# Four reorderings around the stage turns of a hybrid decoder step, and weight steps behind more output units

## The chip, the cores and the metric

The kernel runs on one NeuronCore of a Trainium2 chip. The metric is the device time of one execution in microseconds; lower is better. Before the change it was 2583.95 us (median of 3 runs, 2576.30 to 2586.48 us).

## The reference

One inference step of a decoder trunk of two layers, over 512 prompt tokens and 64 sample tokens (576 columns) with a model width of 1024. All data is fp32.

```python
for l in range(2):
    x = x + 0.5 * gate1 * ffn1(modulate(rmsnorm(x)))     # silu(h Wa) * (h Wb), then W_dn; 2816 wide
    m = mixer(modulate(rmsnorm(x)))                      # one input projection, three branches, W_o
    x = x + gate2 * m
    x = x + 0.5 * gate3 * ffn2(modulate(rmsnorm(x)))
y = rmsnorm(x)
# mixer: sigmoid(ga) * W_A(b * conv3(c * xa)) + sigmoid(gb) * W_B(u * spatial_gate(layernorm(gelu(v))))
#        + sigmoid(gc) * scale * grouped(trailing_mean_w(p) - p), w in (2, 4, 8, 16)
```

Shift, scale and gate come from a projection of a conditioning vector (`w_ada`). Also returned are the last conv and pooling rows and the normalised v rows.

## The kernel before, in words

All work is laid out with features on the 128 partitions and tokens on the free axis, in two halves of 288 columns (256 prompt, 32 sample; h = 0 and h = 1). A product in fp32 is made of three matmuls of a faster type: every operand is split in a high part (`whi`, `hhi`: a rounding copy on ScalarE, ACT) and a low part (`wlo`, `hlo`: a subtraction on VectorE, DVE), and `wlo*hhi + whi*hlo + whi*hhi` is summed in PSUM on TensorE (PE). A *unit* (`units`) is one output block of 128 features and 288 tokens; its bank is then taken over ("evacuated") by ACT or DVE. Most input projections run as *groups* (`Groups.group`): two blocks by two halves in seven products in place of eight, with sums of weight blocks and sums of input blocks (the *moving sums* T1 to T4: `t_sum`, `t_split`, tiles `u`, `thi`, `tlo`).

**What sets the order.** The program is recorded in the order in which the code calls it, with no scheduler: each engine takes its instructions strictly in that order and waits where an operand or a buffer isn't ready. Three counters put side work between products. `beat()` runs what `later(n, f)` has put off by n beats (one per unit or product); `tick()` runs what `after(n, f)` has put off by n units (a product of a group counts a half). `W` holds the weights: raw tiles of 1 MB land by DMA in two buffers, and one *step* at a time splits a block into one of six pairs of buffers (`W.split`, `W.go`, `W.take`), as far as buffers are free. For a group a raw tile takes eight steps: S1 and S3 on GpSimd (POOL; `whi` L360, `raw` L356), S2 and S4 on DVE (`whi`, `raw` L356), and the splits a, c, b, d.

**The turn.** Between two stages the normalisation needs the sum of squares over all 1024 features. `end_stage` ends with four units on h = 0 and four on h = 1. `xupd` evacuates a unit into x (DVE L797 to L805), `square` squares it on ACT and adds it to `accsq`: on POOL, the eighth on DVE (L570). `norm1` sums over partitions on PE (L578) and raises to -1/2 on POOL (L582), `norm2` makes diagonals on DVE (L591 to L593), `norm_bc` spreads them by a matmul with ones (L597), `norm3t` makes the normalised halves: `u` on DVE (L630 to L634), `hhi` on ACT (L637, L639), and in its second part, put off to `run_lo`, `u` on ACT (L645) and `hlo` on DVE (L647). `start_stage` begins with two units on h = 0 whose products with `hlo` come last (`late`, L477), in whose middle (`mid`) h = 1 is normalised; then a third unit, the same on h = 1, a fourth weight block on both halves, and the groups. `t_late` puts off the third and fourth moving sums to the first group's products. There are five turns: into mixer 0, FFN 2 of layer 0, FFN 1 of layer 1, mixer 1 and FFN 2 of layer 1.

Elsewhere in the mixer, `ypair` makes the output projections of branches A and B: four units of four k-blocks for one weight pair. The steps of the `w_ada` projection (`ada_mm`, four matmuls at L514) are spread by `after`.

In a group, ACT copies the first product's bank to `pd` (L749), the third's to `pe` (L760), the fourth's to `pu` (L764); DVE adds the second, fifth and sixth to them (L753, L768, L773). The fourth product writes the bank that `pd` is read from, the fifth the one that `pe` is read from. SiLU of `pd` (L922) is on ACT between them.

Of the kernel before, what the change touches and what calls it, by code (L numbers as in the profile page):

```python
# [15 lines left out]
KT = D // P  # L16
DEPTH = 2
NTOK = 576
HALF = 288
# [16 lines left out]
def kernel(  # L36
# [7 lines left out]
    nc = tc.nc  # L44
# [386 lines left out]
    W = Weights()  # L431
# [23 lines left out]
        while pend:  # L455
            pend.pop(0)[1]()

    def units(specs, hooks={}, late=False, w=1, still=False):


        bk = [balloc() for _ in specs]
        K = specs[0][2]
        for k in range(K):
            for b, (slot, w0, _, rhs, _) in zip(bk, specs):
                whi, wlo = wk(slot, w0 + k)
                rhi, rlo = rhs(k)
                o = b[:, :HALF]
                nc.tensor.matmul(o, wlo, rhi, start=(k == 0), stop=False)  # L468
                if not late:
                    nc.tensor.matmul(o, whi, rlo, start=False, stop=False)  # L470
                nc.tensor.matmul(o, whi, rhi, start=False, stop=(k == K - 1 and not late))  # L471
            if k in hooks:
                hooks[k]()
        if late:
            for k in range(K):
                for b, (slot, w0, _, rhs, _) in zip(bk, specs):
                    nc.tensor.matmul(b[:, :HALF], wk(slot, w0 + k)[0], rhs(k)[1], start=False,  # L477
                                     stop=(k == K - 1))
        for b, s in zip(bk, specs):
            s[4](b)  # L480
            brelease(b)
        if not still:
            beat()
        tick(len(specs) * w)
# [71 lines left out]
    accsq = [None, None]  # L556
    nsq = [0, 0]
    rst = [None, None]

    def square(m, h):  # L560
        c0 = h * HALF
        src = xv(m, slice(c0, c0 + HALF))
        if nsq[h] % 8 == 0:
            accsq[h] = qalloc("accsq")
            nc.scalar.activation(accsq[h], src, AF.Square)
        else:
            s = qalloc("sq")
            nc.scalar.activation(s, src, AF.Square)
            eng = nc.vector if nsq[h] % 8 == 7 else nc.gpsimd
            eng.tensor_add(accsq[h], accsq[h], s)  # L570
            qrelease(s)
        nsq[h] += 1

    def norm1(h):
        nb = nrmbank()
        a = accsq[h]
        for j, c in enumerate((0, 128, 160)):
            nc.tensor.matmul(nb[:, j:j + 1], a[:, c:c + P], inv_d, start=True, stop=True)  # L578
        qrelease(a)
        ve = tmp("ve", 4, 2)  # L580
        nc.vector.tensor_scalar_add(ve[:, :3], nb[:, :3], EPS)
        nc.gpsimd.tensor_tensor(out=ve[:, :3], in0=ve[:, :3], in1=mhalf[:, :3], op=ALU.pow)  # L582
        rst[h] = ve
# [99 lines left out]

    def t_late(n=4):

        for n, (i, f) in enumerate(((3, t_sum), (3, t_split), (4, t_sum), (4, t_split))[:n]):
            for q in range(2):
                later(n + 1, lambda i=i, q=q, f=f: f(i, q))

    def t_free():  # L690
        for i in (1, 2, 3):
# [124 lines left out]
    def start_stage(l, sub, evac, last=4):  # L816

        s = [W.take() for _ in range(2)]

        def mid():  # L820
            norm1(1)
            run_lo(1)
            W.lows()
            run_lo()
            norm2(1)
            norm_ut(1, l, sub)

        run_lo(2)
        units([(s[i], 0, KT, hk(0), evac(i, 0)) for i in (0, 1)], {6: mid}, True)
        nb = norm_bc(1, nrmbank())  # L830
        late_lo.extend(norm3t(1, l, sub, nb))
        s.append(W.take())
        units([(s[2], 0, KT, hk(0), evac(2, 0))])
        run_lo()
        todo = t_early()
        todo.insert(4, lambda: W.pay("AD", 1))

        def some(n):
            for _ in range(min(n, len(todo))):
                todo.pop(0)()  # L840

        units([(s[i], 0, KT, hk(1), evac(i, 1)) for i in (0, 1)], {k: lambda: some(1) for k in range(KT)},
              True)
        W.hold = False
        W.pay()
        W.done()
        W.done()
        units([(s[2], 0, KT, hk(1), evac(2, 1))], {k: lambda: some(1) for k in range(KT)})
        W.done()
        s.append(W.take())  # L850
        some(99)
        for h in (1, 0):
            units([(s[3], 0, KT, hk(h), evac(3, h))])
        W.done()
        t_late(last)

    def end_stage(K, rhs, evac, nxt, first=None):
# [29 lines left out]
        for i in range(4):  # L887
            units([(s[i], 0, K, rhs(1), evac(4 + i, 1))],
                  {K - 1: turn1} if i == 0 else {2: turn3} if i == 2 else
                  {2: lambda: part3(4, 2)} if i == 3 else {})  # L890
            W.done()
            if i == 3:
                part3(6, 2)
            if i == 0:
                W.pay("AD+", 1)

# [103 lines left out]
    def mixer(l, nxt):  # L1000
# [204 lines left out]
        def ypair(rhs, evac, m, first=None):  # L1205
            s = W.take()
            for i in (0, 1):
                for h in (0, 1):
                    units([(s, 4 * i, 4, rhs(h), evac(m + i, h))])
                    if first is not None:  # L1210
                        first()
                        first = None
# [673 lines left out]
```

## Time and profile before

| | |
|---|---|
| time, median of 3 runs (range) | 2583.95 us (2576.30 to 2586.48) |
| time of the profiled execution | 2581.12 us |
| its span | 2579.4 us |
| PE busy | 2499.5 us, 97% |
| DVE busy | 1792.8 us, 70% |
| ACT busy | 1159.0 us, 45% |
| POOL busy | 782.6 us, 30% |
| DMA queue q1 | 300.52 MB, 35.1% of 16 engines |

The span is from the first to the last instruction; 1.7 us of the profiled time lie outside it. Busy shares are means over the whole span. The places where PE waits are few and short, and a list of PE's waits with the engine that ended each says more than the shares.

### The profile page before, as it was taken

The page shows a single profiled execution, that of the slowest core. Times are in us where ns is not written, and L with a number is a line of the kernel's source. Part 1 is how long each engine was busy: PE and PEld are TensorE (multiplying, and loading weights), DVE is VectorE, ACT ScalarE, POOL GpSimd, SP SyncE. Part 2 cuts the span into 40 slices and gives each one's busy share as a digit, 9 for nine tenths or more (in the row PEclk, how much of TensorE's full clock was granted, in tenths as well). Part 3 has the DMA queues.
Part 4 walks back from the last instruction along what each step waited for, and adds up shares of the span by engine and source line. Part 5 has one row for each costly group of instructions (what it writes and reads, how often), then busy time and mean ns, then how long its engine had stood idle before and what let it go on. Part 6 is the DMA issues. An engine that isn't in the chain of part 4 may idle for free. (4 is left out here: it accounts for less than half of the span.)

```text
span 2579.4 us, 46614 instructions
## 1 busy us (share of the span) xinstructions
PE 2499.5 (97%) x18604; PEld 2396.4 (93%) x18604; DVE 1792.8 (70%) x3201; ACT 1159.0 (45%) x2134; POOL 782.6 (30%) x878
## 2 busy tenths in 40 slices
PE   7999999999899999999999999999989999999998
PEld 4898999999899989999988999999989999999998
DVE  5766667666797486766776667766678966776675
ACT  5344335544445354333553344446444544453353
POOL 1233332221442223333222333422125232233230
PEclk9999999999999999999999999999999999999999
DMA  7554533312223334342324453332222331222222
GB/s 243 193 177 171 196 106 110 122 56 87 95 82 116 119 117 146 125 161 97 110 83 164 152 176 132 99 127 85 94 73 85 102 135 46 86 99 83 99 79 82
DMA packets 260551, 303.50 MB, mean 118 GB/s; under 512 B 10836, under 2 KB 215948, under 8 KB 260318
## 3 DMA queue, kind: packets, MB, share of 16 engines
q1 hardware_dynamic: 260334, 300.52, 35.1%
q8 instruction: 147, 2.41, 0.4%
q14 instruction: 70, 0.57, 0.1%
HBM read 292.75 MB, written 7.97 MB: 117 GB/s over the span
## 5 line engine op out<-in xcount | busy, mean ns | idle before, releaser
L324 DVE TENSOR_TENSOR wlo<-raw,whi 128x1024 fp32r<-128x1024 f32 (+2 forms) x578 | 639.6, 1114 | 210.1 <-ACT whi L320 200.8
L320 ACT ACTIVATE whi<-raw 128x1024 fp32r<-128x1024 f32 (+2 forms) x578 | 495.6, 866 | 237.6 <-PE mm L471 100.8
L722 PE MATMUL mm<-hhi,wlo 128*128 128x288 f32 x1920 | 571.7, 298 | 23.3 <-ACT pe L760 10.3
L724 PE MATMUL mm<-hhi,whi 128*128 128x288 f32 x1920 | 566.4, 295 | 0.0
L723 PE MATMUL mm<-hlo,whi 128*128 128x288 f32 x1920 | 566.3, 295 | 0.0
L468 PE MATMUL mm<-ghi,wlo 128*128 128x288 f32 x1408 | 418.7, 297 | 0.0
L471 PE MATMUL mm<-ghi,whi 128*128 128x288 f32 x1408 | 414.9, 295 | 0.0
L470 PE MATMUL mm<-glo,whi 128*128 128x288 f32 x1408 | 414.9, 295 | 0.0
L722 PEld LDWEIGHTS mm<-hhi,wlo 128*128 128x128 f32 x1920 | 361.3, 188 | 48.8 <-ACT pe L760 13.5
L724 PEld LDWEIGHTS mm<-hhi,whi 128*128 128x128 f32 x1920 | 361.5, 188 | 0.0
L723 PEld LDWEIGHTS mm<-hlo,whi 128*128 128x128 f32 x1920 | 361.5, 188 | 0.0
L722 PE MATMUL mm<-thi,wlo 128*128 128x288 f32 x1120 | 333.3, 298 | 2.6 <-ACT pd L749 2.6
L360 POOL TENSOR_TENSOR whi<-raw 128x512 f32<-128x512 f32 x120 | 174.0, 1450 | 522.8 <-DMA raw<-in_w_in_dram 138.4
L723 PE MATMUL mm<-tlo,whi 128*128 128x288 f32 x1120 | 330.4, 295 | 0.0
L724 PE MATMUL mm<-thi,whi 128*128 128x288 f32 x1120 | 329.4, 294 | 0.0
L797 DVE SCALAR_TENSOR_TENSOR x<-mm,mod,x 128x256 f32<-128x256 f32 x336 | 161.1, 480 | 218.7 <-PE mm L471 218.6
L468 PEld LDWEIGHTS mm<-ghi,wlo 128*128 128x128 f32 x1408 | 264.1, 188 | 17.8 <-issue 16.8
L470 PEld LDWEIGHTS mm<-glo,whi 128*128 128x128 f32 x1408 | 264.3, 188 | 0.2
L471 PEld LDWEIGHTS mm<-ghi,whi 128*128 128x128 f32 x1408 | 264.2, 188 | 0.0
L722 PEld LDWEIGHTS mm<-thi,wlo 128*128 128x128 f32 x1120 | 210.0, 187 | 15.4 <-issue 4.2
L724 PEld LDWEIGHTS mm<-thi,whi 128*128 128x128 f32 x1120 | 210.8, 188 | 0.0
L723 PEld LDWEIGHTS mm<-tlo,whi 128*128 128x128 f32 x1120 | 210.3, 188 | 0.0
(315 smaller groups left out, 4692.0 us busy)
## 6 DMA issues: line engine op xcount, KB each, us to landing
raw<-in_w_gu_dram SPq DMA_DIRECT2D x88, 1024.0 KB
ada<-in_w_ada_dram SPq DMA_DIRECT2D x256, 256.0 KB
raw<-in_w_in_dram SPq DMA_DIRECT2D x48, 1024.0 KB
raw<-in_w_dn_dram SPq DMA_DIRECT2D x52, 512.0 KB
raw<-in_w_dn_dram SPq DMA_DIRECT2D x24, 768.0 KB
adap<-in_w_ada_dram SPq DMA_DIRECT2D x32, 256.0 KB
raw<-in_w_o_dram SPq DMA_DIRECT2D x8, 1024.0 KB
xd<-x SPq DMA_DIRECT2D x16, 288.0 KB
```

Source lines behind the costliest of these rows:

```text
L320: nc.scalar.activation(hi, src, AF.Copy)
L324: eng.tensor_sub(lo, src, hi.bitcast(F32))
L360: nc.gpsimd.tensor_add(v4(self.sums[r][0])[:, 0], a21, a22)
L468: nc.tensor.matmul(o, wlo, rhi, start=(k == 0), stop=False)
L470: nc.tensor.matmul(o, whi, rlo, start=False, stop=False)
L471: nc.tensor.matmul(o, whi, rhi, start=False, stop=(k == K - 1 and not late))
L722: nc.tensor.matmul(o, wlo, rhi, start=(start and k == 0), stop=False, skip_group_check=True)
L723: nc.tensor.matmul(o, whi, rlo, start=False, stop=False, skip_group_check=True)
L724: nc.tensor.matmul(o, whi, rhi, start=False, stop=(k == 3), skip_group_check=True)
L797: nc.vector.scalar_tensor_tensor(out=xc, in0=ps[:, :PH], scalar=mod[:, gidx + m, 0:1], in1=xc, op0=ALU.mult, op1=ALU.add)
```

## The change

The diff has four parts. (a) In `square` the eighth sum is put in a list; for h = 1 it is recorded behind the last piece of `norm3t`, for h = 0 in `norm1`. (b) In `mid`, the low part of the third weight block (`W.lows`) is recorded behind the diagonals, and that block's first unit takes its products with `wlo` last (`late="w"`). (c) `t_late` spreads the third and fourth moving sums and their splits over seven beats in place of four. (d) `W.go()` runs one more weight step behind each unit of the fourth block in `start_stage` and behind each unit in `ypair`. In `units`, the new line `w, r = ...` assigns to `w`, which is also the parameter that weighs the unit in `tick(len(specs) * w)` at the function's end: behind a unit with `late="l"` it is 0, with `late="w"` it is 1.

```diff
-    def units(specs, hooks={}, late=False, w=1, still=False):
+    def units(specs, hooks={}, late="", w=1, still=False):
...
-                nc.tensor.matmul(o, wlo, rhi, start=(k == 0), stop=False)
-                if not late:
-                    nc.tensor.matmul(o, whi, rlo, start=False, stop=False)
+                if late != "w":
+                    nc.tensor.matmul(o, wlo, rhi, start=(k == 0), stop=False)
+                if late != "l":
+                    nc.tensor.matmul(o, whi, rlo, start=(late == "w" and k == 0), stop=False)
                 nc.tensor.matmul(o, whi, rhi, start=False, stop=(k == K - 1 and not late))
...
-                    nc.tensor.matmul(b[:, :HALF], wk(slot, w0 + k)[0], rhs(k)[1], start=False,
+                    w, r = (0, 1) if late == "l" else (1, 0)
+                    nc.tensor.matmul(b[:, :HALF], wk(slot, w0 + k)[w], rhs(k)[r], start=False,
...
-            eng = nc.vector if nsq[h] % 8 == 7 else nc.gpsimd
-            eng.tensor_add(accsq[h], accsq[h], s)
-            qrelease(s)
+            def add(eng):
+                eng.tensor_add(accsq[h], accsq[h], s)
+                qrelease(s)
+
+            if nsq[h] % 8 == 7:
+                sqlast.append(lambda: add(nc.vector))
+            else:
+                add(nc.gpsimd)
...
     def norm1(h):
+        while sqlast:
+            sqlast.pop()()
...
-        for n, (i, f) in enumerate(((3, t_sum), (3, t_split), (4, t_sum), (4, t_split))[:n]):
+        for i, f, at in ((3, t_sum, (1, 1)), (3, t_split, (2, 3)), (4, t_sum, (4, 5)), (4, t_split, (6, 7)))[:n]:
             for q in range(2):
-                later(n + 1, lambda i=i, q=q, f=f: f(i, q))
+                later(at[q], lambda i=i, q=q, f=f: f(i, q))
...
         def mid():
             norm1(1)
-            run_lo(1)
-            W.lows()
             run_lo()
             norm2(1)
+            W.lows()
             norm_ut(1, l, sub)
...
-        units([(s[2], 0, KT, hk(0), evac(2, 0))])
+        units([(s[2], 0, KT, hk(0), evac(2, 0))], {}, "w")
...
             units([(s[3], 0, KT, hk(h), evac(3, h))])
+            W.go()
...
                 part3(6, 2)
+                sqlast.pop()()
...
                     units([(s, 4 * i, 4, rhs(h), evac(m + i, h))])
+                    W.go()
```

DVE at the last turn, into FFN 2 of layer 1, before (`nrb` is PE's bank of the norm, `raw` to `wlo` a weight split):

```order
L570 TENSOR_TENSOR accsq_24518<-accsq_24518,sq_24973 128x288
L630 TENSOR_TENSOR u_24845<-u_24845,nrb_24899 128x2x32
L632 TENSOR_TENSOR u_24845<-u_24845,mod 128x2x32
L634 SCALAR_TENSOR_TENSOR u_24845<-x_24253,mod,nrb_24899 128x256 x2
L647 TENSOR_TENSOR hlo<-u_24839,hhi 128x2x288
L647 TENSOR_TENSOR hlo<-u_24841,hhi 128x2x288
L581 TENSOR_SCALAR ve_25023<-nrb_25019 128x3
L647 TENSOR_TENSOR hlo<-u_24843,hhi 128x2x288
L324 TENSOR_TENSOR wlo_24855<-raw_24535,whi_24854 128x1024
L647 TENSOR_TENSOR hlo<-u_24845,hhi 128x2x288
L591 TENSOR_SCALAR diag_25033<-ident,ve_25023 128x128
L592 TENSOR_SCALAR diag_25033<-ident,ve_25023 128x128
```

DVE at the same place after the change (L630 `u` stands just ahead of these rows; line numbers from 464 on are 1 to 11 higher):

```order
L642 TENSOR_TENSOR u_24845<-u_24845,mod 128x2x32
L644 SCALAR_TENSOR_TENSOR u_24845<-x_24253,mod,nrb_24899 128x256 x2
L573 TENSOR_TENSOR accsq_24518<-accsq_24518,sq_24973 128x288
L657 TENSOR_TENSOR hlo<-u_24839,hhi 128x2x288
L657 TENSOR_TENSOR hlo<-u_24841,hhi 128x2x288
L591 TENSOR_SCALAR ve_25023<-nrb_25019 128x3
L657 TENSOR_TENSOR hlo<-u_24843,hhi 128x2x288
L657 TENSOR_TENSOR hlo<-u_24845,hhi 128x2x288
L601 TENSOR_SCALAR diag_25032<-ident,ve_25023 128x128
L602 TENSOR_SCALAR diag_25032<-ident,ve_25023 128x128
L603 TENSOR_SCALAR diag_25032<-ident,ve_25023 128x32
L324 TENSOR_TENSOR wlo_24855<-raw_24535,whi_24854 128x1024
```

The sum of squares has moved behind the last `u`, and the weight's low part from ahead of the last `hlo` to behind the three diagonals. The other four turns have the same two moves.

DVE at the beginning of the first group behind the same turn, before (`glo` and `sil` are the FFN's inner values, `u` L658 the third and fourth moving sums, `pd` the second product's evacuation):

```order
L324 TENSOR_TENSOR wlo_25266<-raw_24673,whi_25265 128x512
L943 TENSOR_TENSOR glo_25294<-sil_25067,ghi_25293 128x288
L658 TENSOR_TENSOR u_25037<-u_25041,u_25037 128x576
L658 TENSOR_TENSOR u_25039<-u_25043,u_25039 128x576
L753 TENSOR_TENSOR pd_25344<-mm_25350,pd_25344 128x288
L676 TENSOR_TENSOR tlo_25365<-u_25037,thi_25364 128x576
L676 TENSOR_TENSOR tlo_25369<-u_25039,thi_25368 128x576
L658 TENSOR_TENSOR u_24843<-u_24843,u_24839 128x576
L658 TENSOR_TENSOR u_24845<-u_24845,u_24841 128x576
L324 TENSOR_TENSOR wlo_25374<-raw_25176,whi_25373 128x1024
L356 TENSOR_TENSOR whi_25329<-whi_25329,raw_25176 128x512
L356 TENSOR_TENSOR raw_25176<-raw_25176,whi_25329 128x4x128
```

And after:

```order
L324 TENSOR_TENSOR wlo_25266<-raw_24673,whi_25265 128x512
L946 TENSOR_TENSOR sil_25067<-mm_25304,sil_25067 128x288
L954 TENSOR_TENSOR glo_25294<-sil_25214,ghi_25293 128x288
L954 TENSOR_TENSOR glo_25294<-sil_25067,ghi_25293 128x288
L668 TENSOR_TENSOR u_25037<-u_25041,u_25037 128x576
L668 TENSOR_TENSOR u_25039<-u_25043,u_25039 128x576
L324 TENSOR_TENSOR wlo_25333<-raw_25176,whi_25332 128x1024
L356 TENSOR_TENSOR whi_25301<-whi_25301,raw_25176 128x512
L356 TENSOR_TENSOR raw_25176<-raw_25176,whi_25301 128x4x128
L763 TENSOR_TENSOR pd_25348<-mm_25356,pd_25348 128x288
L686 TENSOR_TENSOR tlo_25371<-u_25037,thi_25370 128x576
L686 TENSOR_TENSOR tlo_25394<-u_25039,thi_25393 128x576
```

The `wlo` of 512 columns has moved ahead of the last `sil`, and one weight's `wlo`, S2 and S4 ahead of `pd`; the fourth sums have left this stretch. The groups behind the two other FFN turns read the same.

ACT at the same place, before:

```order
L947 ACTIVATE ghi_25293<-sil_25214 128x288
L947 ACTIVATE ghi_25293<-sil_25067 128x288
L749 ACTIVATE pd_25344<-mm_25331 128x288
L675 ACTIVATE thi_25364<-u_25037 128x576
L675 ACTIVATE thi_25368<-u_25039 128x576
L922 ACTIVATE pd_25344<-pd_25344 128x288
L320 ACTIVATE whi_25373<-raw_25176 128x1024
L760 ACTIVATE pe_25389<-mm_25376 128x288
L764 ACTIVATE pu_25408<-mm_25331 128x288
```

And after:

```order
L958 ACTIVATE ghi_25293<-sil_25214 128x288
L958 ACTIVATE ghi_25293<-sil_25067 128x288
L320 ACTIVATE whi_25332<-raw_25176 128x1024
L759 ACTIVATE pd_25348<-mm_25335 128x288
L685 ACTIVATE thi_25370<-u_25037 128x576
L933 ACTIVATE pd_25348<-pd_25348 128x288
L320 ACTIVATE whi_25375<-whi_25301 128x1024
L770 ACTIVATE pe_25391<-mm_25378 128x288
L685 ACTIVATE thi_25393<-u_25039 128x576
L320 ACTIVATE whi_25398<-raw_25176 128x1024
L774 ACTIVATE pu_25413<-mm_25335 128x288
```

A weight's high part stands ahead of the first `pd`, one `thi` has moved from ahead of `pe` to behind it, and a `whi` stands between `pe` and `pu`.

## Rows read from the trace of the kernel before

**Rows 1.** The page, busy time of PE: us, share of span, instructions
```profile
PE 2499.5 (97%) x18604; PEld 2396.4 (93%) x18604; DVE 1792.8 (70%) x3201; ACT 1159.0 (45%) x2134; POOL 782.6 (30%) x878
```

**Rows 2.** Waits of PE: who ended them; us in total, times, longest
```profile
PE mm L722 <- DVE wlo L324: 14.2, 4, 4.5
PE mm L722 <- ACT pe L760: 10.3, 9, 2.3
PE mm L477 <- DVE hlo L647: 6.2, 10, 1.1
PE mm L468 <- ACT hhi L639: 5.7, 5, 1.4
```

**Rows 3.** Timeline of PE, last turn: start, us, instruction, [idle before, releaser]
```profile
2167.85 0.40 PE L468 MATMUL mm<-hhi,wlo 128*128 128x288 f32 x1 [0.71 <-ACT hhi L639]
2172.95 0.80 PE L477 MATMUL mm<-hlo,whi 128*128 128x288 f32 x4 [1.11 <-DVE hlo L647]
...
2201.81 0.40 PE L722 MATMUL mm<-thi,wlo 128*128 128x288 f32 x1 [1.65 <-ACT pd L749]
2206.00 0.40 PE L722 MATMUL mm<-hhi,wlo 128*128 128x288 f32 x1 [2.33 <-ACT pe L760]
```

**Rows 4.** Timeline of PE, first group behind the turn into FFN 1, layer 1
```profile
1358.05 0.61 PE L722 MATMUL mm<-hhi,wlo 128*128 128x288 f32 x1 [2.32 <-ACT pe L760]
```

**Rows 5.** Timeline of DVE, last turn
```profile
2164.64 0.19 DVE L805 TENSOR_TENSOR x<-x,t 128x32 f32<-128x32 f32 x1
2165.47 0.46 DVE L570 TENSOR_TENSOR accsq<-accsq,sq 128x288 f32<-128x288 f32 x1 [0.64 <-ACT sq L568]
2165.85 0.21 DVE L630 TENSOR_TENSOR u<-u,nrb 128x64 f32<-128x64 f32 x1
...
2170.91 1.22 DVE L324 TENSOR_TENSOR wlo<-raw,whi 128x1024 fp32r<-128x1024 f32 x1
2172.05 0.85 DVE L647 TENSOR_TENSOR hlo<-u,hhi 128x576 fp32r<-128x576 f32 x1
```

**Rows 6.** Timeline of POOL around the last turn
```profile
2154.90 1.07 POOL L615 TENSOR_TENSOR u<-x,mod 128x64 f32<-128x64 f32 x4
...
2171.69 1.88 POOL L615 TENSOR_TENSOR u<-x,mod 128x64 f32<-128x64 f32 x4
```

**Rows 7.** Timeline of DVE, first group behind the last turn
```profile
2201.28 0.68 DVE L324 TENSOR_TENSOR wlo<-raw,whi 128x512 fp32r<-128x512 f32 x1
...
2203.58 0.44 DVE L753 TENSOR_TENSOR pd<-mm,pd 128x288 f32<-128x288 f32 x1
...
2206.62 1.21 DVE L324 TENSOR_TENSOR wlo<-raw,whi 128x1024 fp32r<-128x1024 f32 x1
...
2209.15 1.42 DVE L676 TENSOR_TENSOR hlo<-u,hhi 128x576 fp32r<-128x576 f32 x2
```

**Rows 8.** Timeline of ACT, first group behind the last turn
```profile
2203.02 1.35 ACT L675 ACTIVATE thi<-u 128x576 fp32r<-128x576 f32 x2 [1.26 <-DVE u L658]
2204.28 0.43 ACT L922 ACTIVATE pd<-pd 128x288 f32<-128x288 f32 x1
2204.61 1.04 ACT L320 ACTIVATE whi<-raw 128x1024 fp32r<-128x1024 f32 x1
2205.56 0.39 ACT L760 ACTIVATE pe<-mm 128x288 f32<-128x288 f32 x1
```

**Rows 9.** A window over one step of L514: us, busy PE, PEld, granted clock, DMA
```profile
918.84:919.84 1.00, 1.00 (x8) 0.15 (x8) 1.00 0.00 0
```

**Rows 10.** Timeline of DVE and ACT, pooling branch of mixer 0
```profile
619.39 0.46 DVE L753 TENSOR_TENSOR pd<-mm,pd 128x288 f32<-128x288 f32 x1 [2.18 <-PE mm L724]
...
631.09 0.45 DVE L753 TENSOR_TENSOR pd<-mm,pd 128x288 f32<-128x288 f32 x1
...
627.71 0.41 ACT L749 ACTIVATE pd<-mm 128x288 f32<-128x288 f32 x1
```

**Rows 11.** A window: us, busy PE, PEld, DVE, ACT, POOL, granted clock, DMA
```profile
660.20:664.90 4.70, 4.70 (x20) 4.70 (x21) 4.62 (x12) 1.38 (x3) 0.56 (x1) 0.50 0.01 2
```

More of the change, by code (lines that the diff above doesn't have):

```diff
@@ L558 @@
     rst = [None, None]
+    sqlast = []
     def square(m, h):
@@ L821, in mid @@
             norm1(1)
-            run_lo(1)
-            W.lows()
             run_lo()
             norm2(1)
+            W.lows()
             norm_ut(1, l, sub)
         run_lo(2)
-        units([(s[i], 0, KT, hk(0), evac(i, 0)) for i in (0, 1)], {6: mid}, True)
+        units([(s[i], 0, KT, hk(0), evac(i, 0)) for i in (0, 1)], {6: mid}, "l")
         nb = norm_bc(1, nrmbank())
@@ L842, in start_stage @@
         units([(s[i], 0, KT, hk(1), evac(i, 1)) for i in (0, 1)], {k: lambda: some(1) for k in range(KT)},
-              True)
+              "l")
         W.hold = False
```

## The prediction

> **What bounds the kernel now.** I read the page first, then PE's waits, then the places of those waits in the timelines of PE, DVE, ACT and POOL. PE is busy for 2499.5 of 2579.4 us [rows 1]: the change leaves PE its matmuls, so it can only shorten or lengthen what lies between them, some 80 us. The list of waits [rows 2] shows what that is: behind the start-up, a few tens of waits of 0.2 to 4.5 us. Three kinds belong to this change. At the turns PE waits for `hhi` (5.7 us over 5 turns) and for `hlo` (6.2 us, two at each turn). In the first groups behind a turn it waits for ACT's copies `pd` and `pe`, which free the banks: `pe` alone 10.3 us in all the kernel [rows 2], 1.65 + 2.33 us behind the last turn [rows 3]. In the mixers' pooling branch it waits for `wlo` (14.2 us in 4 waits) [rows 2].
>
> The first two kinds are chains through queues that work in order. In the last turn x is complete at 2164.83, but DVE next has the eighth sum of squares, which waits 0.64 us for ACT; the `u` that PE needs begins only at 2165.85 [rows 5]. Four DVE pieces on, the weight's `wlo` (1.22 us) stands ahead of the last `hlo`, for which PE then waits 1.11 us [rows 3, 5].
>
> **The change part by part.**
>
> (a) *The sum behind the norm.* It moves `u` up by 2165.85 - 2164.83 = 1.0 us [rows 5], and with it `hhi` on ACT. That covers a wait of 0.71 us [rows 3] whole; the longest is 1.4 us [rows 2] and keeps 0.4. Two of the five waits are of the short kind, three of the long: 5.7 - 3 x 0.4 = 4.5 us saved. The sum itself now ends some 1.3 us later against `u`, yet PE wants it only after `hhi`, in the middle of the two units; I cost that at nothing, and if the cover went it would be what PE waits for in place of `hhi`, at most the 1.0 us gained.
>
> (b) *The low part behind the diagonals.* The last `hlo` no longer has 1.22 us of `wlo` ahead of it, which is more than the 1.11 us of wait [rows 3, 5]. The later one of the two `hlo` waits at a turn, about 0.25 us, is another block's and stays: 6.2 - 5 x 0.25 = 4.9 us saved. What is late next are the diagonals: `ve` goes over POOL, and by its row-by-row durations they are ready when PE gets there, within some 0.2 us. The `wlo` now stands ahead of the `u` of h = 1, but `u` must first wait for PE's broadcast, so nearly all of it fits in; and the unit that uses it asks for it 16 matmuls later. I take 0.3 us off for these. Together (a) and (b) give 4.5 + 4.9 - 0.3 = 9.1 us. Bounds: 5 us if the diagonals or POOL bind, 11.9 (both waits whole) if everything fits.
>
> At this place POOL counts too: its four products at L615 took 1.07 us by themselves and 1.88 us with DVE at work beside them [rows 6]. The Trainium skill, "SBUF — State Buffer", § Who interferes with whom, says that a DVE instruction with two SBUF inputs contends with a GpSimd instruction that reads SBUF, and that the one issued later is blocked. `wlo` is such an instruction, and now falls right beside these products. By that rule POOL's part could end later by up to a whole `wlo`, 1.2 us per turn, 6 us in all: that is the third rival below, which the 0.8 us between the two rows alone makes possible.
>
> (c) and (d) *in the first group of an FFN.* This is the part that speaks against the change. The two extra `W.go` behind the fourth block bring the steps of the next weight forward by one product; the order rows show what this puts in front of whom. On DVE a `wlo` of 512 columns now precedes the last `sil`, for whose `ghi` ACT waits just ahead of `pd`: 0.60 us. On ACT a `whi` (0.95 us from start to start [rows 8]) precedes `pd`. So `pd` comes 1.55 us later, and PE's fourth product with it. Then DVE's own `pd` has `wlo`, S2 and S4 of the next weight ahead of it, 2209.15 - 2206.62 = 2.53 us [rows 7], from 2203.58 to 2206.1. ACT's SiLU stands behind that `pd` and `pe` behind the SiLU. The spreading of `t_late` gives back one `thi` ahead of `pe`, of which only 0.3 us counted (DVE's `pd` ended at 2204.02, the two `thi` at 2204.37 [rows 7, 8]). So `pe` comes 2.53 - 0.3 = 2.25, rounded 2.3 us later, at 2208.2; and PE, which already waited for it, goes on 2.3 us later. Behind it `pu` now has a `thi` and a `whi` ahead, which I price at 0.4 us beyond the product that hides the rest. Sum 2.7 us for a group behind a turn. The third sums still come in time for the sixth product, the fourth for the tail.
>
> All three FFN turns wait for the same `pe` (2.33 and 2.32 us in two of them [rows 3, 4]), so 3 x 2.7 = 8.1 us. Further, the diff's `w, r = ...` makes the two late pairs count nothing in `tick`, so what `after` schedules comes 4 units later. In two FFN turns a step of L514, 1.0 us of PE [rows 9], stood inside this stretch, where the wait for `pe` swallowed it; now one fewer stands there and 1.0 us is paid elsewhere: + 2 x 1.0. Cost of this part 10.1 us. Bounds: zero (the moved pieces find holes that the rows don't show me) and 3 x 4.5 = 13.5 us. A gain here would be the waits themselves, about 8.6 us: 1.65 + 2.33 + 2.32 in two turns [rows 3, 4] and some 2.3 in the third. I take the 10.1, since it is an addition along in-order queues.
>
> *`W.go` in `ypair`.* Four weight steps stand earlier in a mixer's output projections. DVE has a hole there of 2.18 us ahead of `pd` at 619.39 [rows 10]. What is moved is one `wlo`, S2 and S4, 2.53 us [rows 7]. The pooling work behind it runs without a break to the waits for `wlo`, so it all comes earlier, though not before PE's products: the second group's `pd` at 631.09 could begin when its product ends, about 627.71 + 1.6 = 629.3 [rows 10] (1.6 is 12 matmuls at 0.133). I take 1.7 us per mixer, 3.4 us in two; bounds 0 and 2 x 2.18. Behind the other `ypair`s PE doesn't wait, or waits for DVE pieces whose order stays.
>
> *The clock.* Where PE has stood for 4.5 us [rows 2], the following 4.7 us were granted half the clock, 1.2 GHz in place of 2.4 [rows 11]: 20 matmul records where 35 would fit. The first matmul behind the 2.32 us wait took 0.61 us and the one behind the 2.33 us wait 0.40 [rows 3, 4]: the first fell to half, the second not. Longer waits in the three groups will meet this more often, shorter ones at the turns less. At about 1.6 us each I put one more such fall: +0.7 with the one at a turn that may go. The Trainium skill, "TensorE: Matmul & The Clock Gate", § What's actually happening, says the throttled state is the default and activity releases it; the rows agree, and it gives no other sum.
>
> **Sum.** -9.1 + 10.1 - 3.4 + 0.7 = -1.7 us. Against the profiled execution, 2581.1 us, that is 2579.4. The median of the runs shown is 2.8 us above that execution, so I expect a median of 2583.95 - 1.7, about 2582 us.
>
> **Rivals.**
>
> 1. *The groups don't pay.* If the moved pieces fall into DVE's and ACT's idle time, the 10.1 us and the extra clock fall away: -9.1 - 3.4 = -12.5 us, 2571; with part of the groups' own waits gone too (t_late takes two sums and a `thi` out of the stretch) -21 us, 2563. For it: the diff moves sums away from just these waits. Against it: the order rows put 2.53 us ahead of `pd`, and DVE was busy there without a gap.
>
> 2. *The other side: the clock takes over.* In each FFN group two waits of about 3.3 us would stand 1.6 us apart, as in the pooling branch, where the clock fell for 4.7 us [rows 11]. If it falls at all three, each costs 4.7 / 2 = 2.35 us, +7 in place of +0.7, and with no gain in the mixers the sum is -9.1 + 10.1 + 7 = +8 us, 2592. It decides once two groups fall and the turns save under 7 us.
>
> 3. *The turns save half,* since POOL's products and the diagonals take the place of `hlo`: -4.5 in place of -9.1, so +3 us, 2587.
>
> **How the numbers follow.** A chance of 0.52 for the forecast with its own range of 2575 to 2589, 0.24 for the first rival (0.08 of it for -21), 0.11 for the second, 0.13 for the third. A measurement tells 0.5% from no change, 12.9 us: faster is below 2571.0, slower above 2596.9. The first rival's -12.5 lies on that bound, so half of its 0.16 counts as faster, with the 0.08 of -21 and a little from the forecast: 0.20. Slower needs the second rival and more: 0.06. The rest, 0.74, is no change. The range of 8 in 10 takes in the first rival's near case and the second: 2567 to 2593.
>
> **What would show it.** In the changed profile: the waits for `hhi` at most 0.4 us and the first `hlo` wait gone at all five turns; the sum of squares behind `u` without a wait behind it. In the first groups of the three FFN turns `pd` at about 3 us of wait where none of L514 stands ahead, and `pe` at about 3.3; if these are no longer than before, the step with the pieces ahead of `pd` is wrong. In the pooling branch the waits for `wlo` smaller by 1.7 us in all. If DVE's `u` of h = 1 waits for POOL, the third rival holds. A time below 2571 would mean that the groups' queues were not the bound I took them for.

## The result, and the profile after

The changed kernel takes 2600.34 us (median of 4 runs, 2598.71 to 2601.79) against 2580.12 us before (4 runs, 2575.64 to 2586.48). The ratio is 1.0083 with a 95% interval of 1.0066 to 1.0100: 0.8% slower, about 21 us, where 2 us faster was forecast, and above the range's upper end of 2593. The profiled execution took 2600.66 us with a span of 2599.0 us.

PE's row of the page answers to [rows 1]:

```profile
PE 2518.5 (97%) x18604; PEld 2410.8 (93%) x18604; DVE 1793.1 (69%) x3201; ACT 1158.6 (45%) x2134; POOL 777.9 (30%) x878
```

PE stands idle for 2599.0 - 2518.5 = 80.5 us, as before (79.9). The whole loss is in its busy time, 19.0 us more for the same 18604 matmuls: more of them ran at half clock (mean granted clock 0.985 against 0.993). The idle time, as long as before, is not made of the same waits. The waits of PE after, beside [rows 2]; columns: who waited for whom, us in total, times, longest:

```profile
PE mm L732 <- ACT pe L770: 11.7, 9, 3.3
PE mm L732 <- ACT pd L759: 9.6, 5, 2.7
PE tpb L1086 <- POOL wsn L1044: 7.1, 2, 3.8
...
PE mm L732 <- DVE wlo L324: 5.9, 4, 2.2
...
PE mm L732 <- ACT pu L774: 4.9, 8, 1.6
...
PE mm L479 <- DVE hlo L657: 2.3, 5, 0.6
...
PE mm L469 <- ACT hhi L649: 1.0, 3, 0.3
```

The turns did what was forecast: `hhi` fell from 5.7 to 1.0 us, `hlo` from 6.2 to 2.3 us, and the waits for `wlo` in the pooling branch from 14.2 to 5.9. In their place stand 7.1 us for `wsn`, which was no wait of PE before, 4.9 us for `pu`, and longer ones for `pd` and `pe`.

**The turn.** DVE in the last turn, to be held against [rows 5]:

```profile
2178.29 0.21 DVE L640 TENSOR_TENSOR u<-u,nrb 128x64 f32<-128x64 f32 x1
...
2179.46 0.45 DVE L573 TENSOR_TENSOR accsq<-accsq,sq 128x288 f32<-128x288 f32 x1
...
2184.89 1.21 DVE L324 TENSOR_TENSOR wlo<-raw,whi 128x1024 fp32r<-128x1024 f32 x1
...
2186.26 1.33 DVE L642 TENSOR_TENSOR u<-u,mod 128x64 f32<-128x64 f32 x1
```

`u` no longer stands behind the sum, the sum waits for nobody, and `wlo` lies behind the diagonals. One `u` of h = 1 ran for 1.33 us in place of about 0.2, while POOL was at a weight's sum S1 (`whi` L360, 1.29 us from 2186.22); PE's wait there (0.6 us for `hlo`, 0.2 before) stays small.

**The first group behind a turn.** PE, last turn, beside [rows 3], then ACT and DVE at the same place, beside [rows 7, 8]:

```profile
2216.26 0.61 PE L732 MATMUL mm<-thi,wlo 128*128 128x288 f32 x1 [2.69 <-ACT pd L759]
...
2221.46 0.61 PE L732 MATMUL mm<-hhi,wlo 128*128 128x288 f32 x1 [1.96 <-ACT pe L770]
...
2225.43 0.61 PE L732 MATMUL mm<-thi,wlo 128*128 128x288 f32 x1 [0.72 <-ACT pu L774]
```

```profile
2214.86 1.04 ACT L320 ACTIVATE whi<-raw 128x1024 fp32r<-128x1024 f32 x1
2215.81 0.39 ACT L759 ACTIVATE pd<-mm 128x288 f32<-128x288 f32 x1
...
2219.72 0.44 ACT L933 ACTIVATE pd<-pd 128x288 f32<-128x288 f32 x1 [2.88 <-DVE pd L763]
...
2221.02 0.39 ACT L770 ACTIVATE pe<-mm 128x288 f32<-128x288 f32 x1
...
2224.02 1.06 ACT L320 ACTIVATE whi<-raw 128x1024 fp32r<-128x1024 f32 x1 [2.04 <-DVE wlo L324]
2224.98 0.39 ACT L774 ACTIVATE pu<-mm 128x288 f32<-128x288 f32 x1
```

```profile
2216.70 1.22 DVE L324 TENSOR_TENSOR wlo<-raw,whi 128x1024 fp32r<-128x1024 f32 x1
...
2219.24 0.45 DVE L763 TENSOR_TENSOR pd<-mm,pd 128x288 f32<-128x288 f32 x1
```

`whi` ahead of ACT's `pd`, and `wlo`, S2 and S4 ahead of DVE's (2.54 us from the one row to the other), are the pieces that the forecast put there. The `whi` ahead of `pu` was in it too, but not that this `whi` waits 2.04 us itself, for a `wlo` on DVE. Each of the three first matmuls behind a wait takes 0.61 us in place of 0.40: PE is at half clock. Windows of 12 us from PE's first resumption in the three first groups (columns: us, busy PE, PEld, DVE, ACT, POOL, granted clock, DMA share, GB/s), after, then before:

```profile
936.20:948.20 12.00, 7.09 (x36) 6.51 (x37) 9.40 (x13) 5.73 (x10) 0.00 (x0) 0.76 0.34 109
1361.56:1373.56 12.00, 8.73 (x36) 8.04 (x37) 9.41 (x13) 5.73 (x10) 0.00 (x0) 0.53 0.33 111
2216.26:2228.26 12.00, 9.32 (x36) 8.63 (x37) 9.41 (x13) 5.73 (x10) 0.00 (x0) 0.50 0.06 20
```

```profile
935.34:947.34 12.00, 10.66 (x79) 9.59 (x80) 11.79 (x19) 8.20 (x14) 0.00 (x0) 1.00 0.43 132
1358.05:1370.05 12.00, 12.00 (x80) 11.16 (x80) 10.42 (x16) 7.71 (x15) 1.12 (x1) 0.87 0.44 137
2201.81:2213.81 12.00, 9.67 (x71) 9.43 (x72) 11.89 (x19) 8.20 (x15) 0.00 (x0) 1.00 0.14 45
```

After the change the last one is at 1.2 GHz from end to end. Before, only the second group fell [rows 4].

**The wait that nobody forecast.** POOL and PE in the turn into mixer 0:

```profile
509.87 1.27 POOL L360 TENSOR_TENSOR whi<-raw 128x512 f32<-128x512 f32 x1 [25.08 <-DMA raw<-in_w_in_dram]
511.08 0.64 POOL L1044 TENSOR_SCALAR_AFFINE_SELECT wsn<-wsn 128x512 f32<-128x512 f32 x1
```

```profile
511.79 0.66 PE L1086 MATMUL tpb<-ident,wsn 128*128 128x128 f32 x4 [3.24 <-POOL wsn L1044]
```

And POOL at this place in the kernel before:

```profile
485.62 1.22 POOL L1033 TENSOR_SCALAR_AFFINE_SELECT wsn<-wsn 128x512 f32<-128x512 f32 x2
511.93 1.30 POOL L360 TENSOR_TENSOR whi<-raw 128x512 f32<-128x512 f32 x1 [25.08 <-DMA raw<-in_w_in_dram]
```

The two masks over `wsn`, the spatial weights of the mixer's branch B, are put off by `after`. They stood 25 us ahead of S1 of the next weight (`whi` L360); now the first stands behind it in POOL's queue, and S1 waits for its transfer. So a mask of 0.64 us comes 25 us later, PE's transposes wait for it (3.24 us here, 3.84 in mixer 1), and behind them PE was granted 0.57 of its clock for 4 us here and 0.50 for 5 us in mixer 1.

### The profile page after: what moved, and what is told of

It is laid out like the page before. It is cut to its first block, busy times and chain, and to the rows that moved or that the text cites. A ratio compares the mean times of both kernels' runs of the same rounds, so it can differ in the third digit from the quotient of the medians.

```text
span 2599.0 us, 46634 instructions
## 1 busy us (share of the span) xinstructions
PE 2518.5 (97%) x18604; PEld 2410.8 (93%) x18604; DVE 1793.1 (69%) x3201; ACT 1158.6 (45%) x2134; POOL 777.9 (30%) x878
## 5 line engine op out<-in xcount | busy, mean ns | idle before, releaser
L324 DVE TENSOR_TENSOR wlo<-raw,whi 128x1024 fp32r<-128x1024 f32 (+2 forms) x578 | 632.3, 1100 | 223.1 <-ACT whi L320 212.2
L360 POOL TENSOR_TENSOR whi<-raw 128x512 f32<-128x512 f32 x120 | 178.4, 1486 | 533.4 <-DVE wlo L324 164.0
```

The lines of the kernel that those rows point to most:

```text
L324: eng.tensor_sub(lo, src, hi.bitcast(F32))
L360: nc.gpsimd.tensor_add(v4(self.sums[r][0])[:, 0], a21, a22)
```

## The experiments

Each was timed in 5 rounds beside the kernel before, whose median in them lay between 2577.4 and 2578.8 us. A ratio is that to the kernel before, with its 95% interval. "Weight steps" are the two `W.go()` in `start_stage`.

### Own names for the indices

```diff
-                    w, r = (0, 1) if late == "l" else (1, 0)
-                    nc.tensor.matmul(b[:, :HALF], wk(slot, w0 + k)[w], rhs(k)[r], start=False,
+                    iw, ir = (0, 1) if late == "l" else (1, 0)
+                    nc.tensor.matmul(b[:, :HALF], wk(slot, w0 + k)[iw], rhs(k)[ir], start=False,
```

> The changed kernel, with the two indices of the late pair given names of their own, so that they no longer overwrite the parameter w that counts the finished units. Theory A (two causes): the masks wsn stand again ahead of the weight's whi on GpSimd, which waits for a transfer; so PE's waits of 3.24 and 3.84 us for wsn and the stretches at half clock behind them go, about 11 us, and the mod steps (L516) stand again ahead of the first group, about 2 us more: 2600 - 13 = 2587 us. The waits for pd, pe and pu in the FFNs' first groups stay (2.1, 3.3 and 1.6 us at the second turn). Rival B (one cause, the added weight steps): the wsn waits come from whi being issued earlier and stay; within 2 us of the changed kernel, 2598 to 2600. Rival C (one cause, the count): the first groups suffer from the late mod step too, and their longer waits go with it: 2575 or less.

Measured: 2586.45 us, ratio 1.0030 (1.0018 to 1.0042). No wait for `wsn` is left, and the `pd`, `pe` and `pu` waits stay (the rows are under the next run but one). Theory A; B and C fall. The overwritten parameter alone is worth 0.53% of the change's 0.83%, 13.7 us. Of these, 7.1 us are the waits for `wsn`, and about 4.3 us the half clock behind them (an estimate: PE's busy time times the missing share of the clock, summed over windows of 1 us). The rest was not taken apart: no run moved the masks alone.

### No weight steps in start_stage

```diff
             units([(s[3], 0, KT, hk(h), evac(3, h))])
-            W.go()
```

> The changed kernel without the two weight steps (W.go) behind the units of the fourth block in start_stage; the overwritten count stays. Theory A: pd, pe and pu in the first groups of the three FFNs come back to about what they were before (0.9 to 1.7, 1.3 to 2.3, none), with the half clock behind them gone: three times about 8 us, 2600 - 24 = 2576 us; the wsn waits of 3.2 and 3.8 us stay. Rival B: both go, 2600 - 36 = 2564 us. Rival C: nothing of note goes, 2597 to 2600 us.

Measured: 2584.71 us, ratio 1.0027 (1.0015 to 1.0039): 0.56% or 14.4 us less than the changed kernel. Theory A in direction; its 24 us had the size wrong, since it set all that each turn had lost against the steps. B and C fall. In the first groups `pd` and `pe` wait 0.4 to 1.2 and 2.1 us, `pu` not at all; the waits for `wsn` stay (3.18 and 4.38 us).

### Both edits

> Both edits in one: own names for the indices and no weight steps in start_stage. Theory A: the two gains add, 2600 - 13 - 24 = 2563 us, some 17 us under the kernel before, from the turns (about 10) and the mixers' pooling branch (about 9). Rivals B and C: what the one edit gives already, 2564 (B) or 2575 (C). If the two interact (the mod step that stands in the group hides in its wait once and not twice), up to 4 us less than the sum, 2567.

Measured: 2570.61 us, ratio 0.9966 (0.9955 to 0.9978), faster than before by 0.34%. The two losses lie beside each other: 13.7 us for the count and 16.5 us for the steps one way round, 15.7 and 14.4 the other. Of the sum, 8.8 us of gain remain, not the 17 expected.

The waits for `pe`, `pd` and `pu` with the weight steps (first three rows: own names alone) and without them:

```profile
PE mm L732 <- ACT pe L770: 11.4, 9, 3.3
PE mm L732 <- ACT pd L759: 9.4, 5, 2.7
PE mm L732 <- ACT pu L774: 7.2, 8, 2.1
```

```profile
PE mm L732 <- ACT pe L770: 9.3, 9, 2.1
PE mm L732 <- ACT pd L759: 5.0, 4, 1.5
...
PE mm L732 <- ACT pu L774: 2.2, 5, 0.5
```

That is 28.0 against 16.5 us: 11.5 us of the steps' cost are these three waits, and the other 4 to 5 are not.

### The overwritten count alone

```diff
                 for b, (slot, w0, _, rhs, _) in zip(bk, specs):
+                    w = 0
```

> The kernel before, with one added line that sets w to 0 in the late pairs, as the change does unnoticed; nothing else of the change. Theory A: the masks fall behind whi on GpSimd, PE waits about 3.5 us for wsn at both mixer turns and runs some 4 to 6 us at half clock behind each, and one mod step falls into the first groups of two FFNs: 2580 + 11 + 2 = 2593 us. Rival B: without the added weight steps there is no wait for wsn: 2580 to 2582. Rival C: it gives the whole loss of the change and more, since the turns gain nothing here: 2605 us or above.

Measured: 2588.47 us, ratio 1.0041 (1.0028 to 1.0053): 10.6 us slower than before. PE waits 3.06 and 3.37 us for `wsn`. Theory A, a little smaller; B and C fall: the count makes this wait without any of the other edits.

### Without the steps in ypair

```diff
                     units([(s, 4 * i, 4, rhs(h), evac(m + i, h))])
-                    W.go()
```

> As the run with own names and without weight steps in start_stage (2570.6 us, 0.34% under before), and also without the weight steps behind the units of ypair; the turns' edits and t_late stay. Theory A: in the profile of the run with them each mixer waits about 1.8 us less ahead of and in the pooling branch (pe at 601 us 0.34 in place of 0.70, pe at 646 us none in place of 0.62, wlo 2.19 in place of 2.63, and about 1 us more where a product comes out of half clock), and 0.9 us longer for two new waits for pu; 2570.6 + 2 x 0.9 to 2 x 1.7 = 2572.5 to 2574 us. Rival D (they bring as much as the table of waits of the changed kernel suggests, where wlo waits fell from 7.1 to 3.0 us per mixer): 2570.6 + 8 = 2578.5 us.

Measured: 2573.08 us, ratio 0.9987 (0.9974 to 1.0001). Against the run with them that is 2.5 us by the medians and 5.4 by the ratios, whose intervals overlap. The median is theory A's; D's 2578.5 us would be a ratio of 0.9999, which the interval still holds. D falls by its mechanism: the waits for `wlo` are 10.6 us here and 9.6 with the steps, 1 us and not 8. Of the 8.3 us by which the waits for `wlo` fell in the changed kernel, most has another cause (last section).

### The old beats of t_late

```diff
-        for i, f, at in ((3, t_sum, (1, 1)), (3, t_split, (2, 3)), (4, t_sum, (4, 5)), (4, t_split, (6, 7)))[:n]:
+        for n, (i, f) in enumerate(((3, t_sum), (3, t_split), (4, t_sum), (4, t_split))[:n]):
             for q in range(2):
-                later(at[q], lambda i=i, q=q, f=f: f(i, q))
+                later(n + 1, lambda i=i, q=q, f=f: f(i, q))
```

> As the run with own names and without weight steps in start_stage, but with t_late's sums and splits at their old beats 1, 2, 3, 4; turns and ypair as changed. Theory A: the waits for pe in the first groups come back by 0.2 us each (1.13 and 2.13 to 1.34 and 2.33), those for pd by up to 0.5 us: 2570.6 + 1 to 2 = 2572 us, which is hardly told from none. Rival E (the spreading is what holds the first groups together): + 6 us or more, 2577 us.

Measured: 2570.02 us, ratio 0.9965 (0.9952 to 0.9978), no different from the run with the new beats (2570.61). The waits for `pe` are longer by the 0.2 us expected (1.34 and 2.33 in place of 1.13 and 2.13), which no time shows. E falls.

### The turn's edits alone

> The kernel before with the two edits at the turn alone: the last sum of squares behind the norm, and the weight's low part behind the diagonals with the third block's unit in its new order (own names for the indices); no other edit of the change. Theory A: the waits for hhi and hlo at the five turns fall from 11.8 to about 3.5 us in all, as in the changed kernel (3.3 us): 2578.7 - 8 = 2570.5 us. Rival F (the mixers give back what their turns gain, since the pooling branch waits for DVE, which doesn't come earlier; the gain of three turns of five stays): 2578.7 - 5 = 2573.5 us.

Measured: 2573.19 us, ratio 0.9978 (0.9966 to 0.9990): 5.7 us faster. By the median that is F's time; the interval leaves A open as well. The waits for `hhi` and `hlo` are 4.0 us in all, 3.3 in the changed kernel and 11.9 before; whether the mixers gave some of it back, this run can't tell.

### One weight step in place of two

```diff
             units([(s[3], 0, KT, hk(h), evac(3, h))])
+            if h:
+                W.go()
```

> As the run with own names and without weight steps in start_stage, but with one weight step behind the first of the fourth block's two units (the change has one behind each). Theory A: each step puts its pieces ahead of pd, pe and pu in the first group, so one of two costs about half of the 16 us that both cost (2586.5 - 2570.6): 2578.5 us, with pe waiting about 0.6 us longer than without. Rival G (the first step is hidden beside the second unit's 24 matmuls, and the loss comes once the second pushes wlo, S2 and S4 ahead of DVE's pd): 2570 to 2572.5 us.

Measured: 2586.94 us, ratio 1.0033 (1.0022 to 1.0045), as much as with both (2586.45), and the waits are the same to 0.2 us (`pd` 2.70, `pe` 3.35, `pu` 1.18 us behind the last turn; with both 2.69, 3.35 and 1.36). Both theories fall. ACT's and DVE's rows in the group behind the last turn agree with those of two steps instruction for instruction, so the second step has no effect there. It isn't the number of pieces but the phase: one step more puts `wlo`, S2 and S4 directly ahead of DVE's `pd`, where `u` stood without it.

### Idle matmuls in the waits

```diff
+        def fill(self, n):
+            if n:
+                nb = nrmbank()
+                for _ in range(n):
+                    nc.tensor.matmul(nb[:, :HALF], hhi[:, 0, 0:P], hhi[:, 0, 0:HALF], start=True, stop=True)
...
+            self.fill(n)
             self.product(ak, s["c"], 4, blk(2), False)
```

> The changed kernel with own names (2586.5 us; both weight steps in start_stage stay), and in the first group behind a turn of the three later FFNs PE gets idle matmuls (128x288, into a bank that nobody reads): 6 ahead of the fourth product (waits for pd), 10 ahead of the fifth (pe), 6 ahead of the sixth (pu), 0.8 and 1.3 us at full clock. They add work and no value. Theory A (of the 16 us that the weight steps cost, the waits are 12 and the half clock behind them 4 to 5): the idle matmuls fit into the waits, the granted clock stays at 1.0 over the groups, 2586.5 - 4.5 = 2582 us. Rival J (the clock falls all the same, or no clock is lost there): 2586.5 us, or up to 3 us more where a wait is shorter than its filling.

Measured: 2582.43 us, ratio 1.0012 (0.9999 to 1.0024): 0.18% less than without them (1.0030), 4.6 us by the ratios, whose intervals overlap by 0.06%, and 4.0 by the medians. Windows over the same three groups, own names alone, then with the idle matmuls:

```profile
930.10:942.10 12.00, 9.04 (x48) 7.30 (x49) 9.70 (x14) 5.75 (x10) 0.00 (x0) 0.80 0.35 110
1354.11:1366.11 12.00, 6.99 (x36) 6.41 (x37) 9.41 (x13) 5.73 (x10) 0.00 (x0) 0.77 0.37 115
2200.99:2212.99 12.00, 7.29 (x36) 6.71 (x37) 9.42 (x13) 5.74 (x10) 0.00 (x0) 0.75 0.06 23
```

```profile
930.56:942.56 12.00, 9.85 (x69) 8.37 (x70) 9.70 (x14) 5.74 (x10) 0.00 (x0) 1.00 0.35 109
1353.02:1365.02 12.00, 8.66 (x61) 8.19 (x62) 9.70 (x14) 5.74 (x10) 0.00 (x0) 1.00 0.35 109
2197.91:2209.91 12.00, 9.92 (x60) 9.34 (x61) 9.70 (x15) 5.73 (x10) 0.00 (x0) 0.86 0.06 22
```

Two of three groups stay at full clock, and by its median the kernel is faster with more work on PE. Summed as under "Own names", the clock lost in the three groups is 8.7 us with own names alone, 1.7 with the idle matmuls, and none without the weight steps (an estimate). So 4 us or more of the 16 are the clock, as theory A has it. The Trainium skill, "TensorE: Matmul & The Clock Gate", § What's actually happening, says that the throttled state is the default and activity releases it; the trace agrees, with 1.00 in two groups with the idle matmuls against 0.80 and 0.77 without.

### The SiLU one beat later

```diff
-            later(1, lambda: out(0, 0)(d, d))
+            later(2, lambda: out(0, 0)(d, d))
```

> As the run with own names and without weight steps in start_stage (2570.6 us), and the evacuation of a group's first output (SiLU on ACT, behind DVE's pd) is put one beat later, behind ACT's copy pe. Theory A (pe is late because the SiLU stands ahead of it in ACT's queue and waits for DVE's pd): PE's waits for ACT's pe go, 1.13, 2.13 and 2.12 us in the FFNs' first groups and 0.2 and 1.3 us in the mixers, 5.4 + 3 = 8 us, 2562.5 us; if the next wait is pu, it takes back up to 1 us per group. Rival H (DVE as a whole is late there, and the wait only moves to the next product, for pu or pd): 2568 to 2571 us.

Measured: 2560.16 us, ratio 0.9926 (0.9907 to 0.9945), 10 us less than without it (2570.61). ACT in the first group of FFN 1, layer 1, without and with the edit:

```profile
1345.96 0.39 ACT L759 ACTIVATE pd<-mm 128x288 f32<-128x288 f32 x1
...
1348.65 0.44 ACT L932 ACTIVATE pd<-pd 128x288 f32<-128x288 f32 x1 [0.35 <-DVE pd L763]
...
1349.95 0.39 ACT L770 ACTIVATE pe<-mm 128x288 f32<-128x288 f32 x1
```

```profile
1347.60 0.40 ACT L759 ACTIVATE pd<-mm 128x288 f32<-128x288 f32 x1
...
1350.79 0.39 ACT L770 ACTIVATE pe<-mm 128x288 f32<-128x288 f32 x1
...
1351.65 0.43 ACT L932 ACTIVATE pd<-pd 128x288 f32<-128x288 f32 x1
```

`pe` comes 3.19 us behind `pd` in place of 3.99, and the SiLU no longer waits. H falls. The time is about theory A's, but the waits that were to go did not all go: behind the three turns they are 0.8 us shorter each (0.34, 1.34 and 1.34 us are left), since a `thi` that waits for DVE and a `whi` still stand ahead. In all the kernel PE's waits for ACT's `pe` fell from 9.3 to 3.4 us, and those for DVE's `pe` and for `pu` by 2.9 more: the edit is in every group.

### The weight sums on DVE in the pooling branch

```diff
-                nc.gpsimd.tensor_add(v4(self.sums[r][0])[:, 0], a21, a22)
+                (nc.vector if self.sv else nc.gpsimd).tensor_add(v4(self.sums[r][0])[:, 0], a21, a22)
...
+        W.sv = True
         G.group(evac_p, 0)
         G.group(evac_p, 2)
         G.group(evac_g, 0)
+        W.sv = False
```

(S3 in the same way.)

> As the run with own names and without weight steps in start_stage, but in the mixers' three groups of the pooling branch the sums S1 and S3 of a weight (128x512) run on DVE and not on GpSimd. Theory A (GpSimd's S1 beside DVE makes DVE's instructions there longer, pws 1.39 in place of 0.32 us and wlo 2.31 in place of 1.22): these take their short times, DVE has 0.7 us more of its own per sum and 1.1 us less per meeting; the wait for wlo of 4.5 us in the one mixer becomes about 3, and of 0.8 us in the other stays under 1.5: between -3 and 0 us, 2567.5 to 2570.6. Rival I (the long instructions have another reason): they stay long and DVE gets later by its added sums, 4 x 0.7 us: 2573.5 us.

Measured: 2569.71 us, ratio 0.9971 (0.9958 to 0.9984), the same as without it (0.9966). Half of theory A held: where the first sum had been, `t<-pw,rcnt` took 0.17 in place of 1.29 us. A third sum was recorded one group later, so on GpSimd still; beside it `pws` took 1.38 and `wlo` 2.31 us, and one mixer still waited 4.41 us for `wlo`.

### Both, and one group further

> The run with the SiLU one beat later (2560.2 us), and the sums S1 and S3 on DVE through the pooling branch and one group further, so that the third S1 too, beside which pws took 1.38 and wlo 2.31 us, leaves GpSimd. Theory A (GpSimd at work beside DVE is the reason): pws takes about 0.33 and wlo about 1.22 us there, with at most GpSimd's two small copies left beside DVE; the third sums add 1.4 us of DVE; per mixer where PE waits 4.5 us for wlo it waits about 3.7: 2558 to 2560 us. Rival I (another reason): pws and wlo stay at 1.4 and 2.3 us, and PE waits 6 us there: 2563 us.

Measured: 2558.86 us, ratio 0.9928 (0.9913 to 0.9943), the lowest median of all, though not to be told from 2560.16. The third sum has left GpSimd, `pws` took 0.32 and `wlo` 1.22 us in both mixers (rows in the last section). Theory A; I falls.

## Why the prediction was wrong

| term | forecast, us | measured, us | by |
|---|---|---|---|
| the turns, (a) and (b) | -9.1 | -5.7 (-8.8 to -2.6); waits -8.6 | turn's edits alone; waits |
| steps in `ypair` | -3.4 | -2.5 to -5.4, intervals overlap | with and without |
| spread of `t_late` | -0.3 a group | 0 | old beats |
| weight steps, waits | +8.1 | +11.5 | with and without |
| weight steps, clock | +0.7 | +4 or more | idle matmuls |
| the overwritten count | +2.0 | +13.7 | own names |
| all together | -1.7 | +21 | result |

- *The turns* were right: the sum of squares stands behind `u` without a wait, the waits for `hhi` are at most 0.33 us, and the `hlo` wait of 1.11 us is gone everywhere. The gain in time of the turn's edits alone is smaller than the waits', which lie at the edge of its interval; that difference stays open.
- *The first groups, `pd` and `pe`,* were right too. The step said that pieces ahead in ACT's and DVE's queues put them 1.55 and 2.3 us off. With and without the steps the two waits together differ by 1.25, 2.54 and 2.77 us in the three groups, 6.6 us where 6.9 were forecast; so the first rival falls. (The step's 2.53 - 0.3 is 2.23 and not 2.25; that moves the sum by 0.2 us at most.)
- *`pu`* was the first mis-sized term. The step "`pu` now has a `thi` and a `whi` ahead, which I price at 0.4 us" counted the instruction's duration and not its own wait. The `whi` stands 2.04 us for DVE's `wlo`, and with own names PE waited 2.12, 1.66 and 1.36 us for `pu`: 5.1 us where 1.2 were forecast.
- *The clock* was the second. One more fall of 1.6 us was counted; with three waits in a row all three groups fell (0.76, 0.53 and 0.50), as the second rival said. That rival's own sum, 2592 us, was still too low, because it shares the next error.
- *The count* is the step that failed: "the two late pairs count nothing in `tick`, so what `after` schedules comes 4 units later". The overwritten parameter was seen, but only the L514 steps on PE were followed. What else `after` holds there, the two masks on POOL, was not looked up, nor what the later place puts ahead of them in that queue: an S1 that waits 25 us for a transfer. The term was put at 2.0 us and measured 13.7, of which some 11 are the waits for `wsn` and the half clock behind them. Without it the time was 2586, inside the range, though slower and not faster than before, by the two terms above and the smaller gain at the turns.
- *The mixers' pooling* came near the forecast for the edit itself, although PE's waits there fell by far more; the reason is in the last section.
- *The third rival* (the turns save half, 4.5 us) is not settled by the time: the interval of 2.6 to 8.8 us holds its 4.5, and the forecast's 9.1 lies just outside. The waits speak against it: of 11.9 us, 3.3 are left. POOL's products took 2.13 us beside `wlo`, against 1.88 before [rows 6], and the `u` of h = 1 that ran for 1.33 us stood beside S1, which was not in that rival.

## What to carry to other kernels

When an edit changes a counter, list everything that is scheduled by it, on every engine, and read at each new place which instruction of the in-order queue now stands ahead and what that one waits for: a 0.64 us mask behind a sum that waits for a transfer, once in each mixer, cost 7.1 us of waits and some 4 us of clock, more than all the reorderings won (8.8). Price an instruction put ahead of another by its wait plus its duration, not by its duration. And where PE waits for a short copy, look first at what stands ahead of this copy in its queue: moving the SiLU, and what stands at its place in the other groups, behind `pe` gained more (10 us) than the edits at the turns (5.7).

## What the runs showed of the hardware

**GpSimd and DVE.** Between PE's two waits for `wlo` in the pooling branch DVE has 11 instructions in each of three kernels. The stretch in the kernel before, the changed kernel, and the last run (columns as in the windows above):

```profile
652.29:660.20 7.91, 3.43 (x25) 3.23 (x25) 7.81 (x11) 3.08 (x6) 4.32 (x4) 0.87 0.00 0
```

```profile
655.52:661.26 5.74, 4.96 (x25) 4.76 (x25) 5.64 (x11) 3.08 (x6) 0.70 (x1) 0.70 0.00 0
```

```profile
649.14:654.80 5.66, 4.83 (x24) 4.63 (x25) 5.62 (x11) 3.08 (x6) 0.00 (x0) 0.72 0.00 0
```

DVE takes 7.81 us with 4.32 us of GpSimd's work beside it, and 5.6 us with 0.70 or none. Two instructions make the difference. DVE in mixer 1 of the run "Both edits", GpSimd's S1 there (it begins when a matmul of PE frees its buffer), and DVE in the last run:

```profile
1910.05 1.39 DVE L1297 TENSOR_TENSOR pws<-pws 128x160 f32<-128x160 f32 x1
1911.36 2.31 DVE L324 TENSOR_TENSOR wlo<-whi,whi 128x1024 fp32r<-128x1024 f32 x1
```

```profile
1909.42 1.84 POOL L360 TENSOR_TENSOR whi<-raw 128x512 f32<-128x512 f32 x1 [4.64 <-PE mm L734]
```

```profile
1904.59 0.32 DVE L1298 TENSOR_TENSOR pws<-pws 128x160 f32<-128x160 f32 x1
1904.82 1.22 DVE L325 TENSOR_TENSOR wlo<-whi,whi 128x1024 fp32r<-128x1024 f32 x1
```

These two are 1.07 and 1.09 us longer beside GpSimd's S1 and S3, though of quite different size, and the profile shows this as busy time, not as a wait. The Trainium skill, "SBUF — State Buffer", § Who interferes with whom, says that a DVE instruction with two SBUF inputs contends with a GpSimd instruction that reads SBUF; the trace agrees for these two, and gives the price. Not every instruction that meets a sum pays it: in mixer 0 of the changed kernel S1 began at 660.56 us, four DVE instructions beside it kept their length, and S1 itself took 3.65 us in place of 1.3.

**A slower PE came through sooner.** In the changed kernel PE was granted less of its clock in this stretch (0.70 in place of 0.87), freed that buffer later, and GpSimd's sum fell behind the stretch: PE's second wait ended 5.74 us behind the first, in place of 7.91. Behind it DVE paid after all (`pw` 1.42 us in place of 0.68, `pws` 1.33 in place of 0.21), but there PE was not waiting. That is why PE's wait of 4.5 us was 0.8 there, in one mixer of the run "Both edits", and also in the run with the count alone, which has no steps in `ypair`. In every profile here the wait is 4.4 to 4.5 us where the stretch was granted 0.85 to 0.91, and at most 0.9 us where it was granted 0.73 or less. So it goes with the clock: the run "Both edits" has one mixer of either kind, and from PE's first resumption to POOL's second `acc<-acc,pd` (L1362) it takes 27.9 us in the one and 32.3 us in the other. The profile of the kernel before has the long wait in both mixers and that of the changed kernel in none, which a table of waits from one execution doesn't tell. How often either comes in the timed runs, and whether an edit changes that, no run shows; the terms of 2 to 6 us in the table above are uncertain by it.
